# Four instead of three column pairs as seven block products in each feed-forward input layer, with one weight sum built by ScalarE and an accumulating DMA

## Chip, core and metric

The kernel runs on one core of one Trainium2 chip. The metric is the time of one execution in device microseconds, and lower is better. Three executions of the kernel before gave 2631.84, 2634.01 and 2633.85 us; the median is 2633.85 us.

## What is computed

Two layers of a streaming encoder on 256 tokens with 2048 features. Each layer is feed-forward, mixer, feed-forward, each followed by a residual sum and a LayerNorm. What the change touches is the input half of the feed-forward blocks (four of them in all):

```python
D_MODEL = 2048; SEQ = 256; D_FF = 2 * D_MODEL

def swiglu(x, w_in, w_out):
    a, gate = jnp.split(x @ w_in, 2, axis=-1)
    return (jax.nn.silu(a) * gate) @ w_out

for i in range(DEPTH):                       # DEPTH = 2
    x = layer_norm(ALPHA * x + 0.5 * swiglu(x, *ffn1[i]), *ln1[i])
    x = layer_norm(ALPHA * x + mixers[i](x), *ln2[i])
    x = layer_norm(ALPHA * x + 0.5 * swiglu(x, *ffn2[i]), *ln3[i])
```

All of it is in float32.

## The kernel before

**Number format.** Each operand is split into two float32r parts: `hi`, a cast on ScalarE (ACT), and `lo`, the difference on VectorE (DVE). A product then takes three part products on TensorE (PE): hi·hi, hi·lo and lo·hi. The function `parts` (line 323) makes such a split for weights, one instruction on ACT and one on DVE for 128 x 1024 elements.

**Two ways to multiply by w_in.** Of the 4096 columns of `a` and the 4096 of `gate`, the first 512 of each are computed by `gemm`. The rest is done in two ways. `column` (line 327) computes 128 columns from one weight load of 1 MB (`raw`): two splits, then 16 pairs of matmuls, a 512-wide one (L341) and a 256-wide one (L345). A feature tile needs two columns, one of `a` and one of `gate`; `ffn_in` lists them as `units`. `Seven.run` (line 376) computes 512 columns of `a` and 512 of `gate` together as a 2x2 block product with seven instead of eight block products. The blocks are the two halves of the features times the two halves of the tokens on one side, and the two halves of the features times (a, gate) on the other. It has eight steps i, one per 128 features of a half. A step loads four weight blocks (b12, b11, b21, b22, 1 MB), forms the weight sums `ta` = (b12 - b11, b12 - b22) and `tb` = (b22 - ta[0], b21 - tb[0]) on DVE (line 400), splits b11, (b21, b22), `ta` and `tb`, and multiplies: 7 products of 3 matmuls, all 512 wide (lines 422 to 424). After eight steps the seven sums are combined on DVE (line 434). SEVENS = 3 such groups stand in each feed-forward block, and 4 * (8 - 3) - 4 = 16 feature tiles, or 32 columns, are left to `column`.

**Order of the work.** `between` (line 558) puts one column behind each step of a group, and one more column stands behind the group, so a group goes with nine columns; four columns stand ahead of the first group and one behind the last. The result of a group is multiplied, transposed on TensorE (`gated`, line 470, tiles `gt`) and copied during the next group. The program is written in this order, and a list scheduler then sets the order on each engine; each engine works through its list in order and waits on semaphores.

**Buffers.** All weights pass through three `raw` buffers (8 KB per partition each), loaded by SyncE's queue (SP), each load waiting until the buffer's last reader is done. Splits go to six `whi` and six `wlo` buffers. `ta` and `tb` take turns in the two `sums` buffers. The activations' parts are in `xs`, with a pitch of W = 258 elements, and the block sums of the activations (`Seven.prepare`) are in `s`.

Of the kernel before, what the change touches and what calls it, by code (L numbers as in the profile page):

```python
# [8 lines left out]
F32 = mybir.dt.float32  # L9
F32R = mybir.dt.float32r  # L10
# [6 lines left out]
KT = D // P  # L17
W = T + 2
WARM = 9
FF = 2 * D  # L20
# [3 lines left out]

SEVENS = 3
PARTS = ('', '_columns', '_seven')
# [12 lines left out]
def trunk(ctx: ExitStack, tc: tile.TileContext, a: dict, out: bass.AP):  # L39
# [3 lines left out]
    raws = ctx.enter_context(tc.tile_pool(name="raws", bufs=3))  # L43
    sums = ctx.enter_context(tc.tile_pool(name="sums", bufs=2))
    whis = ctx.enter_context(tc.tile_pool(name="whis", bufs=6))
# [13 lines left out]

    xsq = [res.tile([P, 4, 2, W], F32R, tag=f"xs{q}", name=f"xs{q}") for q in range(4)]  # L60
    xs = [x[:, j] for x in xsq for j in range(4)]
# [33 lines left out]
    nc.vector.reciprocal(rcount, count)  # L95
    vecs = const.tile([P, len(VECS) * KT], F32, name="vecs")

# [115 lines left out]
    class Norm:  # L213
# [3 lines left out]
        def __init__(self, gname, bname):  # L217
            self.g, self.b = gname, bname
            self.sums = res.tile([P, 2, 2 * T], F32, tag="sums", name="sums")
            lo, hi = VECS.index(gname) * KT, VECS.index(bname) * KT  # L220
            gb = vecs[:, lo:lo + 2 * KT].rearrange("p (j t) -> p t j", j=2)
            assert hi == lo + KT
            for q in range(4):
                h, l = (xsq[q][:, :, i, T:] for i in range(2))
                nc.scalar.copy(h, gb[:, 4 * q:4 * q + 4])
                nc.vector.tensor_tensor(out=l, in0=gb[:, 4 * q:4 * q + 4], in1=h.bitcast(F32), op=ALU.subtract)
# [126 lines left out]
    class Seven:  # L353
# [22 lines left out]
        def run(self, w, grp, between):  # L376

            ps = [None] * 7
            half = None
            for i in range(8):  # L380

                raw = raws.tile([P, 4, 512], F32, tag="raw", name="raw")
                nc.sync.dma_start(raw, w[grp, i])
                b11, b2, b22, b21 = raw[:, 1], raw[:, 2:4], raw[:, 3], raw[:, 2]

# [3 lines left out]

                ta, tb = (sums.tile([P, 2, 512], F32, tag="sum", name=n) for n in ("ta", "tb"))  # L390
                if i % 2 == 0:
# [5 lines left out]

                for dst, x, y in ((ta, raw[:, 0:1].to_broadcast([P, 2, 512]), raw[:, 1:4:2]),
                                  (tb[:, 0], b22, ta[:, 0]), (tb[:, 1], b21, tb[:, 0])):
                    nc.vector.tensor_tensor(out=dst, in0=x, in1=y, op=ALU.subtract)  # L400
# [46 lines left out]
    def ffn_in(w_in, w_columns, w_seven, norm, hooks=None):  # L447
# [10 lines left out]
        def settle(ts):  # L458
            for t in ts:
                slot = 16 + t if t < 16 else 32 if t == 31 else t - 16  # L460
                gs[t] = scratch(slot, F32R, f"g{t}").rearrange("p (h n) -> p h n", h=2)
                src = g32[t // 2][:, t % 2 * T:(t % 2 + 1) * T]
                split(gs[t], src, src)
# [94 lines left out]
        def between(i, h):  # L558
            if h == 1 or i == 7:
                unit()  # L560
            if lates and (i, h) == (0, 1):
                lates.pop()()
# [121 lines left out]
    def pooling(p, norm):  # L684
# [5 lines left out]
        def evac_u(grp, nm):  # L690
            def evac(f, ps):
                win = WINDOWS[grp]
                u = tmp.tile([P, T], F32, tag="z", name="u")
                bias = total(u, ps, nm)
# [3 lines left out]
                while n < win:  # L698
                    s2 = tmp.tile([P, T], F32, tag="win", name="win")
                    nc.vector.tensor_copy(s2[:, :n], s[:, :n])  # L700
# [43 lines left out]
    def last(p, norm):  # L744
# [17 lines left out]
        for i, name in enumerate((f'{p}ln3_g', f'{p}ln3_b')):  # L762
            gb = res.tile([P, 4, 2 * W], F32, tag=f"xs{i}", name=f"gb{i}")
            for q in range(4):
# [104 lines left out]
```

## Time and profile before

| | |
|---|---|
| median of 3 executions | 2633.85 us (2631.84 to 2634.01) |
| the profiled execution: its own time / its span | 2632.2 us / 2630.5 us |
| PE busy | 2612.0 us, 99% of the span |
| DVE busy | 2084.0 us, 79% |
| ACT busy | 1518.1 us, 58% |
| POOL busy | 11.9 us |
| granted TensorE clock | 0.999 of full |
| DMA | 499.53 MB, queues' packets 54% of 16 engines' span |

Busy time is the time in which an engine's instructions ran, counted once where they overlap. The matmul rows give the duration of one matmul with the pipelined end of it, which overlaps the next: the distance between two starts, not the duration, is what a matmul costs in a stream. The same holds for DVE and ACT in a smaller measure.

### The profile page before, as it was taken

How to read it: one execution, taken by the hardware profiler on the slowest of the kernel's cores; microseconds unless marked ns; L12 is line 12 of the kernel's file. 1: busy time of each engine (PE TensorE's matmuls, PEld its weight loads, DVE VectorE, ACT ScalarE, POOL GpSimd, SP SyncE). 2: the span in 40 equal slices, each digit the busy share in tenths (PEclk: the TensorE clock that was granted, in tenths of full speed). 3: DMA queues.
4: the chain of work that ended last, by engine and by line, in shares of the span. 5: the costliest groups of instructions: out<-in, count | busy, mean ns of one | idle time of the engine just before them, and what ended most of it. 6: DMA issues, size and time to landing. Idle time of an engine off the chain costs nothing.

```text
span 2630.5 us, 37467 instructions
## 1 busy us (share of the span) xinstructions
PE 2612.0 (99%) x14828; PEld 2277.8 (87%) x14828; DVE 2084.0 (79%) x2798; ACT 1518.1 (58%) x2130; POOL 11.9 (0%) x28
## 2 busy tenths in 40 slices
PE   9999999999999999999999999999999999999998
PEld 8888888899997888888988888889888898888886
DVE  7899967585689989765799897657878799999645
ACT  6565654466576656644666566445555566656432
POOL 0000000000000000000000000000000000000000
PEclk9999999999999999999999999999999999999999
DMA  7555555554455555555455555554555545555653
GB/s 262 187 208 178 206 209 184 187 179 161 156 177 176 202 198 202 199 180 195 171 191 192 192 196 207 190 192 162 203 183 190 188 154 195 200 198 202 230 195 119
DMA packets 71519, 499.53 MB, mean 190 GB/s; under 512 B 7984, under 2 KB 8624, under 8 KB 12080
## 3 DMA queue, kind: packets, MB, share of 16 engines
q1 hardware_dynamic: 70704, 495.05, 53.7%
q8 instruction: 116, 1.90, 0.3%
q0 software_dynamic: 640, 2.10, 0.2%
q14 instruction: 59, 0.48, 0.1%
HBM read 495.02 MB, written 2.10 MB: 189 GB/s over the span
## 4 chain that ended last, share of the span: by engine, by line
PE 94%; DVE 3%; ACT 1%; issue 1%; DMA 0%; SPq 0%; DVEq 0%; ACTq 0%
PE ps L164 21%; PE pc L341 17%; PE ps L167 11%; PE pc L345 9%; PE p L422 5%; PE p L423 5%; PE p L424 5%; PE ps L159 4%; PE ps L158 4%; PE ps L160 4%; PE y L806 2%; PE y L804 2%; PE y L805 2%; DVE wlo L325 1%; PE v L660 1%
## 5 line engine op out<-in xcount | busy, mean ns | idle before, releaser
L141 DVE TENSOR_TENSOR wlo<-raw,whi 128x1024 fp32r<-128x1024 f32 (+1 forms) x498 | 595.9, 1200 | 407.7 <-ACT whi L140 407.2
L140 ACT CAST whi<-raw 128x1024 fp32r<-128x1024 f32 (+1 forms) x498 | 510.1, 1032 | 548.3 <-PE ps L164 336.6
L341 PE MATMUL pc<-xs,whi 128*128 128x512 f32 x2048 | 729.2, 396 | 1.4 <-ACT gw L483 0.7
L345 PE MATMUL pc<-xs,wlo 128*128 128x256 f32 x2048 | 554.9, 281 | 0.0
L164 PE MATMUL ps<-g,whi 128*128 128x512 f32 x1536 | 537.7, 396 | 0.0
L325 DVE TENSOR_TENSOR wlo<-raw,whi 128x1024 fp32r<-128x1024 f32 (+1 forms) x448 | 487.9, 1103 | 39.3 <-ACT whi L324 21.6
L324 ACT CAST whi<-raw 128x1024 fp32r<-128x1024 f32 (+1 forms) x448 | 417.7, 959 | 164.0 <-PE pc L341 110.8
L341 PEld LDWEIGHTS pc<-xs,whi 128*128 128x128 f32 x2048 | 385.1, 189 | 87.3 <-ACT gw L483 2.6
L167 PE MATMUL ps<-g,wlo 128*128 128x256 f32 x1536 | 427.3, 280 | 0.0
L345 PEld LDWEIGHTS pc<-xs,wlo 128*128 128x128 f32 x2048 | 386.7, 189 | 11.4
L164 PEld LDWEIGHTS ps<-g,whi 128*128 128x128 f32 x1536 | 287.1, 188 | 66.8
L167 PEld LDWEIGHTS ps<-g,wlo 128*128 128x128 f32 x1536 | 289.8, 189 | 1.5
L159 PE MATMUL ps<-xs,whi 128*128 128x258 f32 (+1 forms) x768 | 218.3, 284 | 0.0
L158 PE MATMUL ps<-xs,whi 128*128 128x258 f32 (+1 forms) x768 | 217.6, 283 | 0.0
L160 PE MATMUL ps<-xs,wlo 128*128 128x258 f32 (+1 forms) x768 | 216.5, 282 | 0.0
L164 PE MATMUL ps<-xs,whi 128*128 128x512 f32 x512 | 180.2, 398 | 0.6 <-ACT whi L140 0.6
L350 ACT COPY col<-pc 128x512 f32<-128x512 f32 x128 | 75.3, 588 | 151.6 <-PE pc L341 145.3
L422 PE MATMUL p<-whi,s 128*128 128x512 f32 x384 | 150.9, 395 | 0.9 <-ACT col L350 0.7
L423 PE MATMUL p<-whi,s 128*128 128x512 f32 x384 | 149.8, 392 | 0.0
L160 PEld LDWEIGHTS ps<-xs,wlo 128*128 128x128 f32 x768 | 146.2, 190 | 0.0
L159 PEld LDWEIGHTS ps<-xs,whi 128*128 128x128 f32 x768 | 145.4, 189 | 0.2
L158 PEld LDWEIGHTS ps<-xs,whi 128*128 128x128 f32 x768 | 144.6, 188 | 0.0
(196 smaller groups left out, 4120.9 us busy)
## 6 DMA issues: line engine op xcount, KB each, us to landing
raw<-in_l_ffn_w_in_columns SPq DMA_DIRECT2D x128, 1024.0 KB, 4.9
raw<-in_l_ffn_w_out SPq DMA_DIRECT2D x127, 1024.0 KB, 4.8
raw<-in_l_ffn_w_in_seven SPq DMA_DIRECT2D x96, 1024.0 KB, 4.9
raw<-in_l_pool_w_in SPq DMA_DIRECT2D x32, 1024.0 KB, 4.9
raw<-in_l_ffn_w_in SPq DMA_DIRECT2D x28, 1024.0 KB, 4.9
raw<-in_l_sb_w_qkv SPq DMA_DIRECT2D x24, 1024.0 KB, 4.8
raw<-in_l_pool_w_out SPq DMA_DIRECT2D x16, 1024.0 KB, 4.9
raw<-in_l_sb_w_o SPq DMA_DIRECT2D x8, 1024.0 KB, 4.9
```

Source lines behind the costliest of these rows:

```text
L140: nc.scalar.copy(hi[:, i], src)
L141: nc.vector.tensor_tensor(out=lo[:, i], in0=src, in1=hi[:, i].bitcast(F32), op=ALU.subtract)
L158: nc.tensor.matmul(ps[:, :one], hi[:, cs], x[:, 0, :one], start=first, stop=False)
L159: nc.tensor.matmul(ps[:, :one], hi[:, cs], x[:, 1, :one], start=False, stop=False)
L160: nc.tensor.matmul(ps[:, :one], lo[:, cs], x[:, 0, :one], start=False, stop=last)
L164: nc.tensor.matmul(ps.rearrange("p (h n) -> p h n", h=2), hi[:, cs], x, start=first, stop=last)
L167: nc.tensor.matmul(ps[:, :T], lo[:, cs], x[:, 0], start=False, stop=False)
L324: nc.scalar.copy(hi, src)
L325: nc.vector.tensor_tensor(out=lo, in0=src, in1=hi.bitcast(F32), op=ALU.subtract)
L341: nc.tensor.matmul(ps.rearrange("p (h n) -> p h n", h=2), his[k], whole[k], start=k == 0, stop=k == KT - 1)
L345: nc.tensor.matmul(ps[:, :T], los[k], whole[k][:, 0], start=False, stop=False)
L422: nc.tensor.matmul(p, xh, hi, start=i == 0, stop=False)
```

## The change

SEVENS goes from 3 to 4, so in each feed-forward block one more group of seven block products takes the place of eight columns: 24 columns are left instead of 32, and they stand four ahead of the first group and five with each group. In a step, `raw` no longer holds b12. ScalarE writes -b11 and -b22 into `ta`, and a DMA from the queue of GpSimd (POOL), which adds what it reads to what is in the buffer, adds b12 to both halves; `fetch` issues this for step i + 1 at the start of step i. DVE keeps the two instructions for `tb`. `sums` gets a third buffer. The pitch of `xs` becomes 272 elements and `vecs` gets 8 more. To make room, two tags of `tmp` are shared in the pooling mixer (`z` and `win`), and the last feature tile's parts move into the buffer `rb`.

```diff
 W = T + 2
+PITCH = 272
-SEVENS = 3
+SEVENS = 4
...
-    sums = ctx.enter_context(tc.tile_pool(name="sums", bufs=2))
+    sums = ctx.enter_context(tc.tile_pool(name="sums", bufs=3))
...
-    xsq = [res.tile([P, 4, 2, W], F32R, tag=f"xs{q}", name=f"xs{q}") for q in range(4)]
+    xsq = [res.tile([P, 4, 2, PITCH], F32R, tag=f"xs{q}", name=f"xs{q}") for q in range(4)]
...
-    vecs = const.tile([P, len(VECS) * KT], F32, name="vecs")
+    vecs = const.tile([P, len(VECS) * KT + 8], F32, name="vecs")[:, :len(VECS) * KT]
...
+            def fetch(i):
+                raw = raws.tile([P, 4, 512], F32, tag="raw", name="raw")[:, :3]
+                nc.sync.dma_start(raw, w[grp, i][:, 1:])
+                ta = sums.tile([P, 2, 512], F32, tag="sum", name="ta")
+                nc.scalar.activation(ta, raw[:, ::2], AF.Copy, scale=-1.0)
+                nc.gpsimd.dma_start(ta, w[grp, i][:, 0:1].to_broadcast([P, 2, 512]), accum_op=ALU.add)
+                return raw, ta
+
+            ahead_of = fetch(0)
             for i in range(8):
-                raw = raws.tile([P, 4, 512], F32, tag="raw", name="raw")
-                nc.sync.dma_start(raw, w[grp, i])
-                b11, b2, b22, b21 = raw[:, 1], raw[:, 2:4], raw[:, 3], raw[:, 2]
+                raw, ta = ahead_of
+                if i < 7:
+                    ahead_of = fetch(i + 1)
+                b11, b2, b22, b21 = raw[:, 0], raw[:, 1:3], raw[:, 2], raw[:, 1]
...
-                ta, tb = (sums.tile([P, 2, 512], F32, tag="sum", name=n) for n in ("ta", "tb"))
+                tb = sums.tile([P, 2, 512], F32, tag="sum", name="tb")
...
-                for dst, x, y in ((ta, raw[:, 0:1].to_broadcast([P, 2, 512]), raw[:, 1:4:2]),
-                                  (tb[:, 0], b22, ta[:, 0]), (tb[:, 1], b21, tb[:, 0])):
+                for dst, x, y in ((tb[:, 0], b22, ta[:, 0]), (tb[:, 1], b21, tb[:, 0])):
                     nc.vector.tensor_tensor(out=dst, in0=x, in1=y, op=ALU.subtract)
...
-                slot = 16 + t if t < 16 else 32 if t == 31 else t - 16
-                gs[t] = scratch(slot, F32R, f"g{t}").rearrange("p (h n) -> p h n", h=2)
+                g = (res.tile([P, 2 * T], F32R, tag="rb", name=f"g{t}") if t == 31 else
+                     scratch(16 + t if t < 16 else t - 16, F32R, f"g{t}"))
+                gs[t] = g.rearrange("p (h n) -> p h n", h=2)
...
         def between(i, h):
-            if h == 1 or i == 7:
+            if (i, h) in ((1, 1), (3, 1), (5, 1), (7, 0)):
                 unit()
...
-                u = tmp.tile([P, T], F32, tag="z", name="u")
+                u = tmp.tile([P, T], F32, tag="gate", name="u")
...
-                    s2 = tmp.tile([P, T], F32, tag="win", name="win")
+                    s2 = tmp.tile([P, T], F32, tag="half", name="win")
```

The scheduler orders the changed program anew. The first place is the middle of the first group (first feed-forward block). DVE before, where the two sums of a step are made and `ta` is read (a number behind a name is that of one tile):

```order
L400 TENSOR_TENSOR ta_1086<-raw_1084 128x1024 [waits DMAHW0_49,DVE_49]
L325 TENSOR_TENSOR wlo_998<-raw_1084,whi_997 128x512 [waits Activation_49]
L400 TENSOR_TENSOR tb_1087<-raw_1084,ta_1086 128x512 [waits DVE_49]
L325 TENSOR_TENSOR wlo_1040<-raw_1037,whi_1039 128x1024 [waits DMAHW7_49,Activation_49]
L400 TENSOR_TENSOR tb_1087<-raw_1084,tb_1087 128x512 [waits DVE_49]
```

ACT at that place in the changed program, from the negatives of one step to the cast of that step's finished sum:

```order
L388 ACTIVATE ta_1090<-raw_1088 128x1024 [waits DMAHW1_49,DVE_49]
L326 CAST whi_1046<-raw_1040 128x1024 [waits PE_49]
L326 CAST whi_1094<-raw_997 128x512 [waits PE_49]
L326 CAST whi_1094<-raw_1088 128x512
L326 CAST whi_1098<-raw_997 128x1024 [waits PE_49]
L326 CAST whi_1104<-ta_999 128x1024 [waits DMASW4_49,PE_49]
L326 CAST whi_1108<-tb_1093 128x1024 [waits DVE_49,PE_49,Activation_49]
L388 ACTIVATE ta_1135<-raw_1133 128x1024 [waits DMAHW2_49,DVE_49]
L326 CAST whi_1141<-raw_1088 128x1024 [waits PE_49]
L352 COPY col_1083<-pc_1050 128x512 [waits PE_49]
L326 CAST whi_1147<-ta_1090 128x1024 [waits DMASW5_49]
```

The sum has left DVE; between the negatives of `ta_1090` and the cast that reads the sum, nine ACT instructions stand, and the cast waits on a software DMA (DMASW). The second place is the start of the second group, ACT in the changed program:

```order
L388 ACTIVATE ta_1582<-raw_1580 128x1024 [waits DMAHW3_49]
L326 CAST whi_1586<-raw_1580 128x512
L326 CAST whi_1596<-ta_1491 128x1024 [waits DMASW2_49,PE_49]
L496 COPY gw8_1480<-gt_1475 128x512 [waits PE_49]
L326 CAST whi_1600<-tb_1585 128x1024 [waits DVE_49,Activation_49]
L326 CAST whi_1633<-raw_1580 128x1024 [waits Activation_49]
L496 COPY gw9_1487<-gt_1482 128x512 [waits PE_49]
L326 CAST whi_1639<-ta_1582 128x1024 [waits DMASW3_49,DVE_49]
```

Here only six instructions stand between the negatives and the cast. On POOL, whose queue held nothing in this stretch before, the accumulating DMAs of the first group now follow each other, each behind the negatives it waits for and the landing of the DMA that last wrote its buffer:

```order
L389 DMA ta_999<-in_l0_ffn1_w_in_seven 128x2x512 [waits DMASW2_49,Activation_49]
L389 DMA ta_1090<-in_l0_ffn1_w_in_seven 128x2x512 [waits DMASW3_49,Activation_49]
L389 DMA ta_1135<-in_l0_ffn1_w_in_seven 128x2x512 [waits DMASW4_49,Activation_49]
L389 DMA ta_1225<-in_l0_ffn1_w_in_seven 128x2x512 [waits DMASW5_49,Activation_49]
L389 DMA ta_1420<-in_l0_ffn1_w_in_seven 128x2x512 [waits DVE_49,Activation_49]
```

## Rows read from the trace of the kernel before

**Rows 1.** The page: busy times, and the chain that ended last by engine.
```profile
PE 2612.0 (99%) x14828; PEld 2277.8 (87%) x14828; DVE 2084.0 (79%) x2798; ACT 1518.1 (58%) x2130; POOL 11.9 (0%) x28
...
PE 94%; DVE 3%; ACT 1%; issue 1%; DMA 0%; SPq 0%; DVEq 0%; ACTq 0%
```
**Rows 2.** What PE waited for: us in total, times, longest us (the longest and fifth).
```profile
PE p L422 <- ACT col L350: 1.6, 3, 0.8
...
PE p L424 <- DVE wlo L325: 0.6, 2, 0.5
```
**Rows 3.** Timeline of PE (start us, us): three columns begin; first steps; groups two and three.
```profile
59.24 0.63 PE L341 MATMUL pc<-xs,whi 128*128 128x512 f32 x2
...
64.86 0.63 PE L341 MATMUL pc<-xs,whi 128*128 128x512 f32 x2
...
70.47 0.63 PE L341 MATMUL pc<-xs,whi 128*128 128x512 f32 x2
...
76.32 0.40 PE L422 MATMUL p<-whi,xs 128*128 128x512 f32 x1
...
81.18 0.39 PE L422 MATMUL p<-whi,xs 128*128 128x512 f32 x1
...
165.66 0.40 PE L422 MATMUL p<-whi,xs 128*128 128x512 f32 x1
...
256.94 0.40 PE L422 MATMUL p<-whi,xs 128*128 128x512 f32 x1
```
**Rows 4.** Stretches: us, busy by engine (instructions), PEclk, DMA share, GB/s.
```profile
166.00:257.00 91.00, 90.71 (x465) 76.29 (x464) 82.10 (x97) 55.22 (x69) 0.00 (x0) 1.00 0.54 192
806.00:896.00 90.00, 87.93 (x442) 72.87 (x441) 83.91 (x102) 56.91 (x72) 0.00 (x0) 1.00 0.57 199
```
**Rows 5.** Timeline of DVE in the second group: 256, 1024 and 512 elements, then successors.
```profile
161.46 0.41 DVE L524 TENSOR_TENSOR col<-col 128x256 f32<-128x256 f32 x1
161.79 1.21 DVE L400 TENSOR_TENSOR ta<-raw 128x1024 f32<-128x1024 f32 x1
162.92 1.21 DVE L325 TENSOR_TENSOR wlo<-tb,whi 128x1024 fp32r<-128x1024 f32 x1
```
**Rows 6.** Timeline of ACT there: casts of 1024 and 512 elements, a copy, an activation.
```profile
160.72 1.05 ACT L324 CAST whi<-tb 128x1024 fp32r<-128x1024 f32 x1
161.67 0.63 ACT L324 CAST whi<-raw 128x512 fp32r<-128x512 f32 x1
162.19 0.64 ACT L467 ACTIVATE c<-c 128x512 f32<-128x512 f32 x1
...
170.12 0.57 ACT L350 COPY col<-pc 128x512 f32<-128x512 f32 x1
170.59 1.06 ACT L324 CAST whi<-tb 128x1024 fp32r<-128x1024 f32 x1
...
175.46 0.40 ACT L529 ACTIVATE col<-col 128x256 f32<-128x256 f32 x1
175.77 0.60 ACT L324 CAST whi<-raw 128x512 fp32r<-128x512 f32 x1
```
**Rows 7.** Line 766, the only software DMAs of this kernel: durations min/median/max, times.
```profile
L766 POOL DMA_DIRECT2D gb<-in_l_ln_g x4: 546/549/724, 2440.2 to 2442.0; - x4
L766 POOL DMA_DIRECT2D gb<-in_l_ln_b x4: 546/546/548, 2442.6 to 2444.2; - x4
...
DMA to landing us min/median/max: 4.7/9.4/11.8
```
**Rows 8.** DVE before and while POOL issued these eight DMAs (2440.2 to 2444.7 us).
```profile
2437.28 1.22 DVE L141 TENSOR_TENSOR wlo<-raw,whi 128x1024 fp32r<-128x1024 f32 x1
...
2443.83 1.21 DVE L141 TENSOR_TENSOR wlo<-raw,whi 128x1024 fp32r<-128x1024 f32 x1
```
**Rows 9.** Tile p: product matmuls by weight source, ns min/median/max.
```profile
L424 PE MATMUL p<-wlo,s x384: 387/391/502, 78.2 to 2426.2; 128*128 128x512 f32 x192
L424 PE MATMUL p<-wlo,xs x288: 387/394/500, 76.8 to 2426.9; 128*128 128x512 f32 x144
```

More of the change, by code (lines that the diff above doesn't have):

```diff
@@ L223, in __init__ @@
             for q in range(4):
-                h, l = (xsq[q][:, :, i, T:] for i in range(2))
+                h, l = (xsq[q][:, :, i, T:W] for i in range(2))
                 nc.scalar.copy(h, gb[:, 4 * q:4 * q + 4])
@@ L762, in last @@
         for i, name in enumerate((f'{p}ln3_g', f'{p}ln3_b')):
-            gb = res.tile([P, 4, 2 * W], F32, tag=f"xs{i}", name=f"gb{i}")
+            gb = res.tile([P, 4, 2 * PITCH], F32, tag=f"xs{i}", name=f"gb{i}")
             for q in range(4):
```

## The prediction

> **What bounds the kernel now.** I read the page first: TensorE (PE) is busy for 2612.0 us of the span, and the chain that ended last lies on PE for 94% [rows 1]. Then the list of what PE waited for: the longest entry is 1.6 us in total, the fifth 0.6 us [rows 2]. So a microsecond of matmuls saved is a microsecond of time, as long as the engines that prepare weights keep up. How near they are to not keeping up is read from the stretch of one whole group: in 91.0 us DVE is busy 82.10 us (90%), ACT 55.22 us (61%), at a granted clock of 1.00 [rows 4]. That stretch decides the case, because the change takes matmuls out of it and puts new waits into it.
>
> **What PE saves.** From starts of columns at 59.24, 64.86 and 70.47 us, a column costs 5.62 us of PE; a step of seven products runs from 76.32 to 81.18 us, 4.86 us [rows 3]. The second group, with its nine columns and the transposes of the group before it, lasts from 165.66 to 256.94 us, 91.28 us [rows 3]; less 9 x 5.62 = 50.58 it costs 40.7 us by itself. (The first group, which has no transposes yet, comes to 89.34 - 50.58 = 38.8 us, and 8 x 4.86 = 38.9.) Each feed-forward block gives up 8 columns, 44.96 us, and gains a group, 40.7 us: 4.26 us saved, and over four blocks **17.0 us**. With the first group's figure and transposes at nothing it would be 4 x 6.2 = 24.8 us, which is the far end.
>
> **What the preparing engines carry then.** A group of the changed kernel has five columns: 91.28 - 4 x 5.62 = 68.8 us on PE. DVE's instructions follow each other at 1.13 us for 1024 elements and 0.33 for 256 [rows 5]. It loses `ta`, 8 x 1.13 = 9.0 us, and four columns, each two splits, one sum and half a product, 2 x 1.13 + 0.33 + 0.17 = 2.76, so 11.0 us: 82.1 - 20.0 = 62.1 us of 68.8, 90% as before. ACT's instructions follow at 0.95 us for 1024 elements, 0.52 for 512, 0.47 for a copy of 512 and 0.31 for 256 [rows 6]. It gains negatives, priced like a cast of their size, 8 x 0.95 = 7.6 us, and loses four columns at 2 x 0.95 + 0.47 + 0.16 = 2.53: 55.2 + 7.6 - 10.1 = 52.7 us of 68.8, 77% instead of 61%. Neither is over the time that PE takes, so I cost their work at nothing; PE's matmuls hide it. The cover is thin: DVE's idle time in a group goes from 8.9 to 6.7 us.
>
> **What the accumulating DMA costs.** Nothing in this stretch shows one. The nearest rows are the eight plain software DMAs of 256 KB at the end: POOL needs 0.55 us for each, and from issue to landing they take 4.7 us at the least and 11.8 at the most, the last with all the others queued ahead [rows 7]. The first issue is at 2440.2 and the last at 2444.2, so landings run from 2444.9 to about 2456.0: 11.1 us for seven more, 1.6 us per 256 KB beside the loads of weights. One accumulating DMA writes 512 KB in 256 rows: one more 0.55 us of POOL, and 4.7 + 1.6 us to landing, **6.9 us**. Low end: 0.55 + 4.7 = 5.2 us, if twice the rows cost nothing more. High end: 6.9 + 2 x 1.6 = 10.1 us if reading the buffer back doubles the traffic, and 11.8 if the queue is as full as at the end. I take 6.9, since the loads of this stretch use 0.54 of the DMA engines [rows 4].
>
> What waits for it? POOL's queue holds nothing else here; on ACT everything behind the cast of the sum waits, and on DVE everything behind the first `tb`. In the middle of a group nine ACT instructions stand between negatives and cast: three casts of 1024 of weights, two of 512, two casts of sums, another step's negatives and one copy, 6 x 0.95 + 2 x 0.52 + 0.47 = 7.2 us. 6.9 us is covered. At the start of the second group six stand there, 3 x 0.95 + 0.52 + 2 x 0.47 = 4.3 us: the cast is 2.6 us late. ACT has 16.1 us free in a group, and two columns in a row stand on PE at this turn, so I cost it at 2 us over the whole kernel; if it came through to PE in every group it would be 16 x 2.6 = 42 us. The other limit is the buffer: `ta` of step i + 2 takes the place of `ta` of step i. Once round are negatives 0.95, the DMA, the cast with one other ahead of it 1.9, and the split on DVE with one other ahead of it 2.26, so 5.1 us and the DMA; PE takes 2 x 4.86 + 5.62 = 15.3 us for the two steps. That leaves 10.2 us for the DMA.
>
> **The small parts, at nothing each.** SP's queue: the load of step i + 1 goes ahead of the column's load of step i, and a group loads 8 x 0.75 + 5 = 11 MB in 68.8 us instead of 17 in 91.3, with 4 MB for the accumulating DMAs. Pitch: matmuls whose weights come from `xs` (pitch 258) have a median of 394 ns, those from `s` 391 [rows 9]; 3 ns on 72 such in each of 16 groups is at most 3.5 us gained, and no row shows a loss. DVE relieved at the start of the second block, where PE idles for 2.07 of 90 us [rows 4]: up to 2 us gained. One column instead of two behind the last group: the combination's last sum, the activation and the product, all of 512 elements and below 0.63 us, come to under 2 us, and the column that is left covers 5.62; if not, up to 4 x 2 = 8 us lost. The shared tags in the pooling mixer delay copies that PE does not wait for now.
>
> Sum: 2632.2 (the profiled execution's own time) - 17.0 + 2 = **2617 us**. The median of the runs is 1.65 us above that execution and inside their spread of 2.2 us, so I leave it.
>
> **Rivals.** *The sum lands too late (slower).* If the DMA takes longer than the 10.2 us that the buffer's round leaves, each microsecond over is lost once in two steps, 4 times a group, 64 times in all; from 10.5 us on the kernel is slower than before. At 11.8 us: 2632.2 - 17 + 64 x 1.6 = 2717 us. Milder, lateness at the groups' turns alone: 2632.2 - 17 + 42 = 2657 us. For it: the upper end of the rows reaches it. Against: the queue was full there, and here one or two are under way. Chance 0.19, the milder form likelier.
>
> *DVE becomes the bound (about the same).* If the idle time that DVE has in a group, 8.9 us, is what its waits on ACT and PE need and doesn't shrink, a group takes 62.1 + 8.9 = 71.0 instead of 68.8 us: 16 x 2.2 = 35 us, 2650 us; with half of it 2633. For it: DVE is at 90% before and after, and ACT, which it waits for, is fuller. Against: PE's waits are so few now. Chance 0.17, mostly near the half.
>
> *POOL and DVE block each other (slower).* If each issue of 1.1 us stops DVE, it carries 62.1 + 8 x 1.1 = 70.9 us, 2.1 over PE's: 16 x 2.1 = 34 us, 2649 us. Against it: splits on DVE took 1.21 us while POOL issued and 1.22 before [rows 8]. Chance 0.04. The Trainium skill (SBUF — State Buffer, "Who interferes with whom") has the rule behind this one: a VectorE instruction with two SBUF inputs contends with a GpSimd instruction that reads SBUF. By that rule DVE's splits would stretch in this stretch; the rows beside the eight issues do not show it, so the trace speaks against it for this kind of issue.
>
> *The change doesn't shorten PE's list*, so that 2632 stays: the order of the changed program has 8 fewer columns and one group more per block, so I give it no chance of its own.
>
> **How the numbers follow.** My forecast, 2607 to 2627 us, has 0.60: from 17 us saved to the far end with the pitch, and up to 10 us of small waits. Late sums 0.19, DVE 0.17, POOL 0.04. A measurement of this kernel can tell about 0.2%, 5.3 us, from no change. Faster by more: 0.60 and a quarter of DVE's case, 0.64. Within: half of DVE's case and a little of the late sums', 0.11. Slower: 0.25. The range goes from 2606 (24.8 us saved and 1 to 2 of the pitch) to 2658, the milder late sum; beyond it lie some 0.12 above and 0.03 below.
>
> **What the profile will show.** Right: columns 96 with 5.6 us each, 16 groups, the second to third group's start 68 to 70 us apart, DVE near 90% and ACT near 77% in that stretch, software DMAs landing in 5 to 9 us, PE's waits in all below 6 us. Late sum: `tb` on DVE and the cast of `ta` on ACT waiting on the software queue in most steps, and PE waiting on `whi` and `wlo` of `ta` and `tb`. DVE bound: DVE above 95% in the groups. Blocking: splits on DVE above 1.3 us. I am wrong if groups take 71 us or more, or if PE's matmuls change their pace.

## The result, and the profile after

The changed kernel takes **2802.39 us** (median of 4, 2798.44 to 2811.39), the kernel before 2633.93 us beside it: ratio 1.0646, 95% interval 1.0633 to 1.066. The forecast was 2617 us with a range to 2658; the time lies 144 us above the range: the kernel is slower, where faster was forecast. The profiled execution took 2803.65 us, its span is 2801.8 us.

The page of the changed kernel: busy times, the DMA queues (packets, MB, share of 16 engines), the chain by engine, and DMA issues (KB each, median us to landing).

```profile
PE 2665.4 (95%) x14508; PEld 2248.1 (80%) x14508; DVE 2078.5 (74%) x2818; ACT 1666.4 (59%) x2294; POOL 167.0 (6%) x156
...
q1 hardware_dynamic: 70704, 461.49, 48.3%
q0 software_dynamic: 35456, 69.21, 14.5%
...
PE 48%; issue 20%; DMA 16%; DVE 12%; ACT 3%; POOL 0%; SPq 0%; DVEq 0%; POOLq 0%; ACTq 0%
...
raw<-in_l_ffn_w_in_columns SPq DMA_DIRECT2D x96, 1024.0 KB, 5.9
raw<-in_l_ffn_w_in_seven SPq DMA_DIRECT2D x128, 768.0 KB, 4.4
ta<-in_l_ffn_w_in_seven POOLq DMA_DIRECT2D x128, 512.0 KB, 7.5
```

Against [rows 1], PE's share of the chain falls from 94% to 48%, and DMA rises from 0 to 16%. The software queue moves 69 MB in 14.5% of the DMA engines' time, the loads 461 MB in 48.3%: a byte of the accumulating DMA occupies them twice as long as a byte of a load (14.5 / 69.21 against 48.3 / 461.49).

The first three groups as stretches (columns as in [rows 4]), cut at the first product of each:

```profile
76.70:152.00 75.30, 69.67 (x330) 56.95 (x329) 53.49 (x61) 44.56 (x53) 7.25 (x6) 0.98 0.66 184
152.00:229.80 77.80, 72.62 (x338) 55.28 (x337) 63.88 (x77) 53.27 (x65) 10.89 (x9) 1.00 0.78 205
229.80:305.50 75.70, 71.71 (x337) 55.38 (x336) 60.76 (x74) 50.85 (x62) 9.69 (x8) 1.00 0.79 209
```

A group takes 75 to 78 us where 68.8 was forecast, and neither DVE (64 of 78) nor ACT (53) is full: the engines wait for each other. What ACT, DVE and SP's queue waited for (us in total, times, longest):

```profile
ACT whi L326 <- DMA ta<-in_l_ffn_w_in_seven: 180.5, 56, 7.1
...
ACT ta L388 <- DMA raw<-in_l_ffn_w_in_seven: 68.9, 42, 5.1
...
DVE tb L412 <- DMA ta<-in_l_ffn_w_in_seven: 174.9, 62, 6.4
...
SPq L386 <- DVE tb L412: 496.4, 58, 13.0
SPq L386 <- DVE wlo L327: 284.1, 65, 9.7
```

L388 is the negatives, L389 the accumulating DMA, L386 a step's load. The chain of the stretch from 80 to 125 us shows how these waits hang together (start us, us, what; short pieces left out):

```profile
85.22 7.19 DMA raw<-in_l_ffn_w_in_seven
...
92.49 1.06 ACT ta L388
93.56 0.94 ACT whi L326
...
94.52 0.52 DVE wlo L327
...
95.78 6.74 DMA raw<-in_l_ffn_w_in_seven
...
105.88 6.72 DMA raw<-in_l_ffn_w_in_seven
```

A step's load takes 7 us in this stretch (the median of all is 4.4) and lands; ACT, which has stood at the head of its queue for it, makes the negatives; only behind them comes a cast for the step before; DVE's split of it is the last reader of a raw buffer; then SP issues the next load into that buffer. That is 10.1 us for a step (95.78 to 105.88). PE needs 68.8 / 8 = 8.6 us.

This stretch shows one way in which the round closes, not the commonest. In the chain of the whole execution, by line, the sum's landing has 13% and a step's load 3%:

```profile
PE ps L166 20%; DMA ta<-in_l_ffn_w_in_seven 13%; PE ps L169 10%; DVE wlo L327 5%; DMA raw<-in_l_ffn_w_in_seven 3%; PE ps L160 3%; PE ps L162 3%; PE ps L161 3%; PE y L817 2%; PE y L819 2%; PE y L818 2%; ACT whi L326 2%; DVE tb L412 2%; DVE g L110 1%; DVE wlo L143 1%
```

Elsewhere, then, it is more often the landing that `tb` and the cast of `ta` wait for (174.9 and 180.5 us above); and a fifth of the chain ("issue", 20%) is time for which the profile shows no releaser.

### The profile page after: what moved, and what is told of

It is laid out like the page before. It is cut to its first block, busy times and chain, and to the rows that moved or that the text cites. A ratio compares the mean times of both kernels' runs of the same rounds, so it can differ in the third digit from the quotient of the medians.

```text
span 2801.8 us, 37510 instructions
## 1 busy us (share of the span) xinstructions
PE 2665.4 (95%) x14508; PEld 2248.1 (80%) x14508; DVE 2078.5 (74%) x2818; ACT 1666.4 (59%) x2294; POOL 167.0 (6%) x156
## 3 DMA queue, kind: packets, MB, share of 16 engines
q1 hardware_dynamic: 70704, 461.49, 48.3%
q0 software_dynamic: 35456, 69.21, 14.5%
## 4 chain that ended last, share of the span: by engine, by line
PE 48%; issue 20%; DMA 16%; DVE 12%; ACT 3%; POOL 0%; SPq 0%; DVEq 0%; POOLq 0%; ACTq 0%
PE ps L166 20%; DMA ta<-in_l_ffn_w_in_seven 13%; PE ps L169 10%; DVE wlo L327 5%; DMA raw<-in_l_ffn_w_in_seven 3%; PE ps L160 3%; PE ps L162 3%; PE ps L161 3%; PE y L817 2%; PE y L819 2%; PE y L818 2%; ACT whi L326 2%; DVE tb L412 2%; DVE g L110 1%; DVE wlo L143 1%
## 5 line engine op out<-in xcount | busy, mean ns | idle before, releaser
L143 DVE TENSOR_TENSOR wlo<-raw,whi 128x1024 fp32r<-128x1024 f32 (+1 forms) x498 | 595.7, 1201 | 408.6 <-ACT whi L142 407.8
L343 PE MATMUL pc<-xs,whi 128*128 128x512 f32 x1536 | 544.6, 397 | 0.3 <-ACT whi L326 0.3
L347 PE MATMUL pc<-xs,wlo 128*128 128x256 f32 x1536 | 417.6, 282 | 8.2 <-DVE wlo L327 7.7
L343 PEld LDWEIGHTS pc<-xs,whi 128*128 128x128 f32 x1536 | 289.0, 190 | 64.7 <-ACT whi L326 3.6
L347 PEld LDWEIGHTS pc<-xs,wlo 128*128 128x128 f32 x1536 | 291.5, 191 | 23.8 <-DVE wlo L327 15.7
L434 PE MATMUL p<-whi,s 128*128 128x512 f32 x512 | 212.7, 416 | 57.5 <-ACT whi L326 46.1
L326 ACT CAST whi<-ta 128x1024 fp32r<-128x1024 f32 x128 | 134.3, 1049 | 183.7 <-DMA ta<-in_l_ffn_w_in_seven 180.5
L389 POOL DMA_DIRECT2D ta<-in_l_ffn_w_in_seven x128 | 155.2, 1213 | 1238.7 <-ACT ta L388 960.0
L412 DVE TENSOR_TENSOR tb<-raw,ta 128x512 f32<-128x512 f32 x128 | 88.1, 688 | 177.2 <-DMA ta<-in_l_ffn_w_in_seven 174.9
L436 PE MATMUL p<-wlo,s 128*128 128x512 f32 x512 | 196.9, 411 | 8.8 <-DVE wlo L327 7.5
L435 PE MATMUL p<-whi,s 128*128 128x512 f32 x512 | 202.5, 395 | 0.0
L434 PEld LDWEIGHTS p<-whi,s 128*128 128x128 f32 x512 | 96.7, 189 | 114.0 <-ACT whi L326 79.8
```

Of the source, the lines that this page charges most:

```text
L143: nc.vector.tensor_tensor(out=lo[:, i], in0=src, in1=hi[:, i].bitcast(F32), op=ALU.subtract)
L326: nc.scalar.copy(hi, src)
L343: nc.tensor.matmul(ps.rearrange("p (h n) -> p h n", h=2), his[k], whole[k], start=k == 0, stop=k == KT - 1)
L347: nc.tensor.matmul(ps[:, :T], los[k], whole[k][:, 0], start=False, stop=False)
L434: nc.tensor.matmul(p, xh, hi, start=i == 0, stop=False)
```

## The experiments

Four theories stood at the start. **Order**: the negatives stand ahead of casts that free raw buffers, and wait there for a load. **Traffic**: the accumulating DMA takes DMA engines from the loads. **Late sum**: the sum lands after it is wanted. **Columns**: five columns a group are too much, whatever makes the sum. Times are medians, each beside runs of the kernel before (2632 to 2634 us); the interval is that of the ratio.

**1. The sum back on VectorE** (four groups, pitch and buffers kept).

```diff
-                nc.scalar.activation(ta, raw[:, ::2], AF.Copy, scale=-1.0)
-                nc.gpsimd.dma_start(ta, w[grp, i][:, 0:1].to_broadcast([P, 2, 512]), accum_op=ALU.add)
...
+                for dst, x, y in ((ta, raw[:, 0:1].to_broadcast([P, 2, 512]), raw[:, 1:4:2]),
...
```

> Four of eight column pairs, pitch and shared buffers stay; the whole step load (4 x 512 columns) and the sum ta on VectorE come back as before the change, without ScalarE's negatives and without the accumulating DMA. The changed kernel takes 2802 us, 168 above the kernel before. Order theory (ScalarE's negatives wait at its head for the next load and hold up the casts that free the raw buffers), traffic theory (the accumulating DMA stretches the loads) and late-sum theory (the sum lands after it is wanted) all put the loss on the new way of the sum: this kernel should lie at 2620 to 2665 (17 us saved by TensorE, and up to 2.3 us a group in 16 groups given back to VectorE, which then has some 71 us of work in a group of 69). Column theory (five groups' columns pressed into fewer slots are too much for VectorE and the raw buffers whatever makes the sum): it stays above 2740.

2706.29 us (1.0266 to 1.0297): between the two answers. The second and the third group as stretches:

```profile
142.60:218.50 75.90, 71.64 (x337) 58.41 (x337) 73.36 (x87) 46.79 (x56) 0.00 (x0) 0.96 0.55 194
218.50:287.30 68.80, 68.50 (x338) 56.50 (x337) 67.61 (x79) 42.21 (x53) 0.00 (x0) 1.00 0.52 184
```

DVE is busy 73.36 of 75.90 us and 67.61 of 68.80: with all sums on it, it is the bound. So taking `ta` off DVE is needed for four groups; but the way the change takes it off costs 96 us more than that.

**2. No accumulating DMA** (its line removed).

> The changed kernel without the accumulating DMA: the sum ta is ScalarE's negatives alone, so b12 is left out of three of the seven products' weights. Order theory: little changes, 2770 to 2805, because the negatives still stand ahead of the casts and wait for the next load; the spacing of steps stays near 10 us. Traffic theory: step loads fall from 5.6 to about 4.5 us and the time to 2620 to 2670. Late-sum theory: ScalarE's and VectorE's waits for ta (177 and 184 us idle) go, 2620 to 2700, with the step loads as slow as they are.

2631.45 us (0.9986 to 1.0005). The order theory falls in its plain form: negatives at the same place in ACT's queue cost nothing by themselves. All of the 171 us to 2802 hang on the DMA. And without it the kernel is still no faster than before, though 17 us of matmuls are gone; that is run 7's question. SP's issues in the first group, of the changed kernel and of this one (start us, length of the row; "x2" is two issues, the second 0.33 us ahead of the row's end):

```profile
77.61 7.93 SPq L386 DMA_DIRECT2D raw<-in_l_ffn_w_in_seven  x2
87.56 0.33 SPq L332 DMA_DIRECT2D raw<-in_l_ffn_w_in_columns  x1
95.78 10.43 SPq L386 DMA_DIRECT2D raw<-in_l_ffn_w_in_seven  x2
108.21 0.33 SPq L332 DMA_DIRECT2D raw<-in_l_ffn_w_in_columns  x1
```

```profile
76.61 8.15 SPq L386 DMA_DIRECT2D raw<-in_l_ffn_w_in_seven  x2
86.77 0.33 SPq L332 DMA_DIRECT2D raw<-in_l_ffn_w_in_columns  x1
92.22 7.90 SPq L386 DMA_DIRECT2D raw<-in_l_ffn_w_in_seven  x2
102.13 0.33 SPq L332 DMA_DIRECT2D raw<-in_l_ffn_w_in_columns  x1
```

With three buffers a load is issued when the one three loads earlier has been read out. The step load of 85.21 gives its buffer to the one of 105.88: 20.7 us. Without the DMA the one of 84.43 gives it to that of 99.79 (92.22 + 7.90 - 0.33): 15.4 us. These are single pairs. By counting alone, three of a group's 13 loads take 3/13 of its time, whatever the cause: 17.4 to 18.0 us in the groups of 75.3 to 77.8 us above, 15.6 in one of 67.5. So the spacing describes the round and does not prove that it is the cause; run 8 tests that.

**3. An eighth of the sum** (the DMA adds 64 of each 512 columns).

> The changed kernel, but the accumulating DMA adds only 64 of each 512 columns (b12 is left out of the other 448 of each of the two halves), with the same number of issues and the same waits. Order theory: 2770 to 2805. Traffic theory: one eighth of the traffic, so most of the loss goes: 2630 to 2680 and step loads near 4.5 us. Late-sum theory: what counts is from issue to landing; if that stays at 6 us or more, 2760 to 2805, if it falls to 3 us, below 2700, with it.

2659.78 us (1.009 to 1.012). With the same issues and waits, but little traffic, 143 of the 171 us go. Issue to landing falls too, so this doesn't tell traffic from lateness (min/median/max of the changed kernel, then of this run):

```profile
DMA to landing us min/median/max: 6.0/7.5/10.6
```

```profile
DMA to landing us min/median/max: 3.0/3.9/8.7
```

**4. The same traffic, nobody waits** (the DMA adds into two buffers that no one reads, behind GpSimd copies of one column).

> The changed kernel, but the accumulating DMA goes into two buffers that nobody reads (two DMAs of 256 KB a step, each behind a GpSimd copy of one column of the load), so b12 is left out of three of the seven products' weights. Without any accumulating DMA this kernel took 2631 us, with all of it 2802. If the loss is traffic (the accumulating DMA takes the DMA engines from the loads), it comes back though nobody waits for the sum: 2740 to 2805, with step loads near 5.6 us. If the loss is that ScalarE and VectorE wait for the landing, the time stays at 2630 to 2660, with step loads slow or not.

2735.20 us (1.0346 to 1.0456). Loads are slower than in the changed kernel (5.9 us against 4.4 for steps, 6.8 against 5.9 for columns), and most of the loss is back. But the run is not clean: GpSimd's copies wait for the DMAs and held raw buffers themselves, as SP's queue shows:

```profile
SPq L389 <- POOL dum L393: 83.9, 22, 9.1
SPq L332 <- POOL dum L393: 56.7, 20, 8.0
```

So it bounds the share of traffic alone from above, at 104 us of 171, if these waits only add time.

**5. Copy in place of add** (`accum_op` left out).

> The changed kernel, but GpSimd's DMA copies b12 over the negatives instead of adding it (the negatives are lost from the sum), same bytes, same waits. If adding costs the DMA engines more than copying: landing falls from 7.5 us to 5 us or less, the queue's share from 14.5% to near 8%, and the time to 2640 to 2720. If bytes alone count: landing 7 us or more, 2780 to 2810.

2717.28 us (1.0307 to 1.034): at the upper end of the first answer. Landing is 6.2 us, a little above what was expected, and the queue's share shows what adding costs:

```profile
q0 software_dynamic: 19072, 69.21, 9.3%
```

The same 69.21 MB take 9.3% of the DMA engines instead of 14.5%, in little more than half the packets. Adding is worth 85 us here, copying the same bytes 86.

**6. Sum later; loads earlier.** Two changes of order. In the first, the negatives and the DMA are written behind the splits of the present step. In the second, the load is written two steps ahead, and the negatives behind the present step's first casts.

```diff
+                if i < 7:
+                    ta_next = begin(i + 1, raw_next)
```

> The changed kernel, with the next step's load issued where it is now, but the negatives and the accumulating DMA written behind the splits of the present step (the scheduler puts most of them behind the cast of ta). Order theory: ScalarE no longer stands at the negatives while casts wait, so the part of the loss that stands there goes: below 2750. Late-sum theory: the sum is now started later and is wanted just as early, so the waits for ta grow by some 2 to 3 us a step, 2802 to 3100. Traffic theory: no change, 2790 to 2815.

2938.24 us (1.1143 to 1.1177): the late-sum answer. Starting the sum later only makes DVE wait longer for it (221 us for the DMA's landing, and 116 with no releaser seen).

```diff
-                raw, ta = ahead_of
-                if i < 7:
-                    ahead_of = fetch(i + 1)
+                raw, ta = raws_of[i], ta_next
+                if i < 6:
+                    raws_of.append(load(i + 2))
```

> The changed kernel in full, with each step's load written two steps ahead and the negatives and the accumulating DMA one step ahead, behind the present step's first casts. If the loss is the round load, negatives, casts, split, buffer free, next load: the load leaves that round and the time falls to 2680 to 2770. If it is the landing of the sum or the traffic as such: 2790 to 2830.

2862.06 us (1.0848 to 1.0885), worse than either answer. A step's load that is issued earlier holds one of three buffers for longer, and now the columns' loads come too late (in the changed kernel ACT waits 1.9 us for them):

```profile
ACT whi L326 <- DMA raw<-in_l_ffn_w_in_columns: 199.4, 46, 7.8
```

This points at the buffers and not at the order of the loads; run 8 tests it.

**7. The end of the stage.** The kernel of run 2, with one column less inside the last group. First tried with the column of place (7, 0):

> The kernel with ScalarE's negatives and no accumulating DMA (2631 us; b12 left out of three of the products' weights), with one column of the last group moved behind the group, so that two stand there as before the change. Tail theory: the four stalls of 5.6 us from column to transpose at the end of the four stages are what ate the 17 us of TensorE's saving: 2607 to 2616. Rival (the column is only moved, its time is not won): 2628 to 2633.

2630.75 us (0.9982 to 1.0002), no change, because the edit changed little: that column stood behind the last products already. Then with the column of (5, 1):

```diff
-            if (i, h) in ((1, 1), (3, 1), (5, 1), (7, 0)):
+            if (i, h) in ((1, 1), (3, 1), (5, 1), (7, 0)) and ((i, h) != (5, 1) or len(units) > 3):
```

> The kernel with ScalarE's negatives and no accumulating DMA (2631 us; b12 left out of three of the products' weights), with the third column of the last group moved behind its products, so that three columns stand between the last product and the transposes, as before the change (two in the changed kernel and in the run before this one). Tail theory, cover: the stall of 5.3 us of TensorE at the end of each of the four stages goes, 2607 to 2616. Rival, VectorE sets the tail (it is busy for all 17.0 us from the last product to the transposes): the stall only shrinks, 2622 to 2633.

**2602.99 us** (0.9873 to 0.9902). The end of the first stage, from the last product on, in the kernel before, in run 2 (three stretches) and here:

```profile
336.10:353.40 17.30, 17.30 (x100) 15.11 (x100) 17.30 (x30) 12.30 (x23) 0.00 (x0) 1.00 0.58 194
```

```profile
334.30:345.20 10.90, 10.90 (x64) 9.46 (x63) 10.90 (x19) 9.68 (x18) 0.00 (x0) 1.00 0.64 216
345.20:351.30 6.10, 0.86 (x4) 0.64 (x4) 6.10 (x10) 1.87 (x3) 0.00 (x0) 0.72 0.68 252
351.30:356.30 5.00, 5.00 (x22) 4.29 (x21) 3.14 (x7) 1.88 (x4) 0.00 (x0) 0.66 0.74 269
```

```profile
329.30:346.20 16.90, 16.90 (x99) 14.84 (x99) 16.90 (x26) 12.03 (x21) 0.00 (x0) 1.00 0.77 269
```

In all three DVE is busy for 17 us without a gap until the product that the transposes wait for. PE has three columns there before the change (x100 matmuls), two in run 2 (x64), three here (x99). With two it idles for 5.2 us in each of four stages (run 2's wait of the transposes, L493, for the product):

```profile
PE gt L493 <- DVE c L485: 21.0, 4, 5.2
```

After the first of these stalls it runs at a granted clock of 0.66 (between its levels of 1.2 and 2.4 GHz), where it was 1.00 before. In all, 21 us of idling cost 28 us.

The columns theory falls here too: with five columns to a group and no DMA, the second group takes 67.5 us, less than the 68.8 that were forecast, and PE is busy for all of it.

```profile
143.10:210.60 67.50, 67.50 (x337) 56.68 (x336) 62.40 (x76) 51.63 (x63) 0.00 (x0) 1.00 0.51 173
```

**8. A fourth raw buffer** (the full changed kernel), paid for by five instead of six buffers for casts and for splits; and the same five with three raw buffers.

```diff
-    raws = ctx.enter_context(tc.tile_pool(name="raws", bufs=3))
+    raws = ctx.enter_context(tc.tile_pool(name="raws", bufs=4))
```

> The changed kernel in full, with four raw buffers in place of three, paid for by five buffers in place of six for the casts and for the splits. Round theory (three raw buffers tie the next load to the splits of a step that waits behind the negatives): 2690 to 2770. If the wait for the sum's landing sets the pace: 2790 to 2830. Five buffers for the halves may cost by themselves; a time above 2830 says that they do.

2670.95 us (1.0133 to 1.0163): 131 us back, more than the round theory's answer.

> The changed kernel in full, with five buffers in place of six for the casts and for the splits, three raw buffers as it has. It is the run with four raw buffers less that fourth buffer (2671). If the raw buffer gave the 131 us back: 2795 to 2840 here, the halves cost nothing or a little. If fewer halves gave it back (a shorter queue of casts ahead of their products): 2665 to 2730.

2835.34 us (1.075 to 1.078): five halves by themselves cost 33 us. The two kernels differ by the fourth buffer alone: **164 us**. With it, loads are slower (6.9 and 5.4 us, with three buffers 5.7 and 4.4) and the sum lands little sooner; but both are waited for less, because SP can issue one load sooner. Issues and then DVE's wait for the sum, with four buffers:

```profile
raw<-in_l_ffn_w_in_columns SPq DMA_DIRECT2D x96, 1024.0 KB, 6.9
raw<-in_l_ffn_w_in_seven SPq DMA_DIRECT2D x128, 768.0 KB, 5.4
ta<-in_l_ffn_w_in_seven POOLq DMA_DIRECT2D x128, 512.0 KB, 7.0
```

```profile
DVE tb L412 <- DMA ta<-in_l_ffn_w_in_seven: 14.5, 11, 4.2
```

DVE's wait for the sum goes from 252.7 us (five halves, three raw buffers) to 14.5, at a landing of 7.0 us instead of 7.8. So the sums were late mainly because their loads were issued late. Some 39 us above run 2 are left; what the five halves, the slower loads and the negatives' place each have in them was not separated.

**9. Three groups with the new sums** (SEVENS = 3, nine columns a group).

> The changed kernel with three groups of nine columns, as before the change, and the sums as the change makes them (ScalarE's negatives and the accumulating DMA a step ahead, three raw buffers). Round theory: a round of 10.2 us fits into the 11.4 us that a step has here (91.3 us a group, eight steps), so nearly nothing is lost: 2628 to 2655. If the accumulating DMA costs something whatever the step's time (its traffic, its landing): three quarters of 171 us, 2730 to 2780.

2740.42 us (1.0394 to 1.0433). The round theory misses, and the other answer has the time: 10.2 us should have fitted into 11.4. SP's issues suggest that the round must be counted in loads, not in steps:

```profile
81.36 0.33 SPq L386 DMA_DIRECT2D raw<-in_l_ffn_w_in_seven  x1
91.29 0.33 SPq L332 DMA_DIRECT2D raw<-in_l_ffn_w_in_columns  x1
93.63 0.33 SPq L386 DMA_DIRECT2D raw<-in_l_ffn_w_in_seven  x1
104.04 0.33 SPq L332 DMA_DIRECT2D raw<-in_l_ffn_w_in_columns  x1
```

Here a column's load comes with every step, the three buffers carry 17 loads a group instead of 13, and a step takes 12.3 us (81.36 to 93.63). This run alone does not tell that from a DMA that costs something whatever the step's time.

**10. GpSimd makes the sum** (whole loads, no negatives, no DMA, three columns at the end).

```diff
+                nc.gpsimd.tensor_tensor(out=ta, in0=raw[:, 0:1].to_broadcast([P, 2, 512]), in1=raw[:, 1:4:2], op=ALU.subtract)
```

> Candidate for a faster kernel, all of the computation in it: four groups, whole loads a step ahead, the sum ta by one GpSimd subtraction of 1024 columns in place of ScalarE's negatives and the accumulating DMA, three columns behind the last products. If GpSimd needs less than a step (8.4 us) and leaves VectorE its pace (a split of 1024 columns 1.22 us): 2607 to 2640. If its work stretches VectorE's operations: VectorE has 62 us of work in a group of 67.5, so from a stretch of a tenth on it sets the pace, 2660 to 2750.

2795.46 us (1.0605 to 1.0637): the second answer. GpSimd needs 3.2 us for a sum, well under a step, and DVE's splits stretch (mean ns; the first row is of the changed kernel):

```profile
L327 DVE TENSOR_TENSOR wlo<-raw,whi 128x1024 fp32r<-128x1024 f32 x320 | 384.0, 1218 | 26.9 <-ACT whi L326 26.6
```

```profile
L327 DVE TENSOR_TENSOR wlo<-raw,whi 128x1024 fp32r<-128x1024 f32 x320 | 458.1, 1453 | 0.0
L327 DVE TENSOR_TENSOR wlo<-raw,whi 128x512 fp32r<-128x512 f32 x128 | 158.0, 1236 | 0.5 <-ACT whi L326 0.5
L143 DVE TENSOR_TENSOR wlo<-raw,whi 128x1024 fp32r<-128x1024 f32 x478 | 582.5, 1222 | 386.8 <-ACT whi L142 386.0
```

This is what the Trainium skill says (SBUF — State Buffer, "Who interferes with whom": GpSimd's reads and a VectorE instruction with two SBUF inputs contend). The rows agree with it: 1218 to 1453 ns in the groups, while splits of the same size in the other stages of the same run (L143) keep 1222. GpSimd's DMA issues do nothing of the kind. In the changed kernel a split that begins during one takes no longer than others:

```profile
93.92 1.21 POOL L389 DMA_DIRECT2D ta<-in_l_ffn_w_in_seven  x1 [9.34 <-ACT ta L388]
94.52 1.23 DVE L327 TENSOR_TENSOR wlo<-raw,whi 128x1024 fp32r<-128x1024 f32 x1 [2.83 <-ACT whi L326]
```

**11. What adds up.** Pitch and moved buffers alone, in the kernel before:

> The kernel before (three groups, VectorE makes all sums) with the pitch of 272 and the moved buffers alone. In the trace of the changed kernel's variants a column's pair of matmuls starts every 0.348 us, before 0.354; 16 pairs a column and 128 columns make 12 us. If the pitch (or the alignment that comes with it) is what shortened them: 2619 to 2624. If it is something else in those runs: 2631 to 2635.

2636.73 us (1.0005 to 1.0022): nothing gained, if anything 0.1% lost. The trace shows one place of loss: from 800 to 1000 us, in the second feed-forward block, PE is busy for 193.54 us at a granted clock of 0.98, before 197.64 at 1.00. The cover at the end, in the full changed kernel:

> The changed kernel in full with three columns behind the last group's products in place of two. Without the accumulating DMA this was worth 28 us. If the end of the stage is a term of its own: 2770 to 2785. If the round swallows it (the column taken from the last group leaves its steps as slow as they are, or the group has less to cover its waits): 2790 to 2810.

2772.17 us (1.0511 to 1.0546): 30 us, so it is a term of its own. Four raw buffers and the cover:

> The changed kernel in full with four raw buffers, five of each half, and three columns behind the last group's products. If round and tail are separate terms: 2671 less 16 to 28 us, 2640 to 2656. If with four raw buffers the tail is already covered by the loads that run ahead (the stall there was still 3.2 to 4.1 us of 6.2): 2660 to 2672.

2663.39 us (1.0101 to 1.0137): only 7.6 us less than with the fourth buffer alone, where the runs of the two overlap (2658 to 2671 and 2668 to 2675); with it the end was partly covered.

**12. Two tries at a faster kernel.** VectorE makes `ta` in four of eight steps, with the cover that did not work in run 7; then in two of eight, on top of four raw buffers and the working cover.

> Candidate for a faster kernel, all of the computation in it: four groups, VectorE makes ta in the even steps (whole load), ScalarE and the accumulating DMA in the odd ones, and two columns behind the last group. VectorE then has some 4 x 1.1 us less a group than with all sums on it (71 us), under TensorE's 67.5; the accumulating DMA half of its traffic. If traffic and VectorE were each over their limit by a little: 2605 to 2640. If the accumulating DMA costs even in half its number: 2660 to 2720.

2739.48 us (1.039 to 1.0423), above both answers.

> Candidate for a faster kernel, all of the computation in it: the run before this one (four raw buffers, three columns at the end), with VectorE making ta in two of eight steps (the group's first and fifth, whole loads), so six accumulating DMAs a group. VectorE then has some 264 us of work in a stage of 270, the DMA engines a quarter less of the accumulating traffic, and the group's first sum is not waited for. If what is left is the sum's traffic and the wait at the group's turn: 2615 to 2640. If VectorE is then too close to its limit: 2645 to 2690.

2666.20 us (1.0114 to 1.0156): the range of the second answer, but not its reason. Its second and third groups take 70.8 and 72.3 us with DVE busy for 64.2 and 66.9, so VectorE isn't full; what sets their pace was not found. No full version of the new sums beat the kernel before.

## Why the prediction was wrong

By its own steps; its own sign of being wrong, groups of 71 us or more, was there (75 to 78).

- **What bounds the kernel, and what PE saves (17.0 us): right in sign, too small.** With the DMA out of the way and the end covered, 29 us are saved. Of the 12 us above the forecast, some 5 can be a faster pace of the columns: a pair of matmuls starts 0.351 us after the last one before the change (5.62 / 16, [rows 3]) and 0.348 in that run, by the median, and 96 columns of 16 pairs at 0.003 are 4.6 us (the expectation of the pitch-alone run took 0.354 for the pace before, which the starts don't bear out). The rest was not traced.
- **DVE and ACT, at nothing: right.** Groups of run 7 take 67.5 us with DVE busy about 62, as worked out (68.8 and 62.1). The rival "DVE becomes the bound" is what happens if `ta` stays on DVE (run 1).
- **The accumulating DMA, 6.9 us to landing: nearly right, in part by luck** (7.5; POOL's issue 1.21 us, not 1.1). The rows were of plain DMAs; a plain one of this size lands in 6.2 us (run 5), and the 1.3 us that adding costs stood only in the step's high end. A landing of 7.5 us is under the 10.2 us that the `ta` buffers leave. By that step the DMA would have cost 2 us; it cost 171.
- **SP's queue, "at nothing": the step that failed.** It counted megabytes and found fewer than before; in loads it was no relief, 13 in 68.8 us or one in 5.3, before 17 in 91.3 or one in 5.4. It did not follow the raw buffer through its round. In the kernel before, a raw buffer is free once DVE has split and subtracted it. In the changed one it is taken a step ahead, for the negatives, and kept until `tb`, which reads it, has the sum back from the DMA: one more landing of 7.5 us and one issue of 1.2 within each holding. By the two holdings of run 2, 13 loads through three buffers take 13 x 15.4 / 3 = 67 us without the DMA, and 13 x 20.7 / 3 = 90 us with it; the groups took 75 to 78, since other pairs are shorter (77.61 to 95.78 is 18.2). The same step put the DMA's traffic at 4 MB a group; at twice a load's engine time per byte it also slows the loads (columns 4.9 us without the DMA, 5.9 with it; steps up to 7.2 in the chain above), which lengthens the same round. The step that was put at nothing is, with the landing that falls into the same round, the 171 us. Runs 2, 3, 5 and 8 show it together: remove the DMA, -171; an eighth of its bytes, -143; copy instead of add, -85; one more raw buffer, -164 against its control.
- **The end of the stage, "under 2 us, if not, 8 lost": mis-sized.** It cost 28 us (run 7) to 30 (run 11). The step priced the path of three instructions of 512 elements, and left out what stands before them on DVE: 17 us without a gap (the stretches of run 7). Two columns cover 11 of them, three cover all. The step also counted two columns there before the change and one after it; there were three and two (x100 and x64).
- **Pitch and tags, at nothing: right for the time** (run 11); the pace of the columns does change with them, 0.348 us a pair.
- **Rivals.** "The sum lands too late" had the right place, DVE at `tb` and ACT at the cast of `ta`, and the wrong price, because it named the `sums` buffers as the limit and put the threshold at a landing of 10.2 us. The trace puts little on these buffers: the negatives, which write into them, waited 14.9 us for a split of DVE to be done and 68.9 us for their load. With four raw buffers it is 32.8 us, and no run with more `sums` buffers was made. "POOL and DVE block each other" did not happen with DMA issues; it does with GpSimd arithmetic (run 10).

The sum by what was measured: 2632 - 29 + 28 + 171 = 2802 us. It closes by construction, since the terms are differences of the same runs; that the end is a term of its own is what run 11 adds (30 us beside 28).

What stays open: how the 171 us divide between slower loads and the sum's landing. Run 4 bounds the first at 104 us, run 3 leaves 28 with a landing of 3.9 us and little traffic, but both work through the same buffers. Nor is the lower clock taken apart: the mean granted clock was 0.986 in the changed kernel and 0.995 in run 2, at most 0.009 x 2802 = 25 us of the 171 by an estimate from these two figures.

## What to carry to other kernels

When a step is moved ahead or a slow producer is put between a load and its last reader, list what holds each buffer from issue to last read, and compare holding time x loads / buffers with the time of the group, before the change and not from its trace, where the two agree by counting; a queue can move fewer bytes and still be late. Before giving up work that stands at the end of a stage, see how long the other engines are busy without a gap from the last product to what the next stage waits for: that, not the path of the last few instructions, is what must be covered. A transfer that adds is not a copy with a flag: here it cost 85 us more.

## What was not expected of the hardware

- The accumulating DMA of 512 KB occupies the DMA engines 1.6 times as long as a plain software DMA of the same bytes (14.5% of 2801.8 us against 9.3% of 2718.5), in 1.9 times the packets. The Trainium skill (DMA: Bandwidth & Descriptors, "Anatomy of one DMA — SWDGE (gpsimd) path") gives 2.0 us plus bytes / 436e3 for a software DMA: an estimate of 3.2 us by that page. The traces differ: 6.2 us for the copy and 7.5 us for the add, median, beside the weight loads.
- GpSimd's issue of it takes 1.21 us, of the plain copy 0.72.
- One idle stretch of 5.2 us on PE was followed by a granted clock of 0.66 over the next 5 us.
